# First pair's sums, operand pacing, value stores and late stores moved in a two-layer encoder step

## The chip, the cores and the metric

The kernel runs on one core of a Trainium2 chip. The core has five engines, each with its own in-order queue of instructions: PE (TensorE, matmuls), DVE (VectorE), ACT (ScalarE), POOL (GpSimd) and SP (SyncE, which here only starts transfers). An instruction that has to wait holds back all that stands behind it on its engine. Transfers between the chip's large memory (DRAM below) and the on-chip buffers are started by an engine's queue and run beside the engines. The metric is the device time of one execution in microseconds, the median of three runs.

## The reference

One step of a two-layer streaming encoder on 2048 prompt tokens and 32 sampled tokens, width 1024, in float32. Layer one is a gated delta-rule layer, layer two a banded attention with shared keys and values.

```python
def delta_layer(x, ...):
    proj = x @ w_in                                   # q, k, v, z, a, b
    qkv, new_buf = causal_conv(proj[..., :CONV_DIM], conv_buf, conv_w)
    ...
    o, s_new = gated_delta_rule(q, k, v, g, beta, s0)
    o = o * rsqrt(mean(o * o) + RMS_EPS) * norm_w * silu(z)
    return layer_norm(DN_ALPHA * x + o @ w_out, ln_g, ln_b), new_buf, s_new

def shared_kv(h, w_kv, pos):
    kv = h @ w_kv
    return rope_partial(kv[..., :B_KVW], pos), kv[..., B_KVW:]

def swa_layer(x, k, v, pos, cached, w_in, sinks, w_out, ln_g, ln_b):
    proj = x @ w_in                                   # q and the gate z
    q = rope_partial(proj[..., :B_QW], pos) * (B_HD ** -0.5)
    z = proj[..., B_QW:]
    o = cached_attention(q, k, v, sk) if cached else banded_attention(q, k, v, sk)
    return layer_norm(DN_ALPHA * x + (o * silu(z)) @ w_out, ln_g, ln_b)
```

## The kernel before

Every matrix product in float32 is made of three products of rounded parts: an operand x is split into x_hi (a cast on ACT) and x_lo = x - x_hi (a subtraction on DVE or POOL), and TensorE adds hi·hi, lo·hi and hi·lo. By the trace the stages follow each other: P1 (the first projection with its convolution, to about 690 us), Delta (the delta rule in 17 chunks, to about 1110), O1 (the out-projection with its normalization, to about 1335), P2 (the second projection, q, k, v and gate, about 1310 to 1765) and the attention with its out-projection (to the end).

**O1** takes 17 tiles of 128 tokens (the last has 32). For each, `O1.tiles` fetches the gated output g of the next tile (`g<-s_g`, L1156) and the rows of x (L1161) on SP, splits g (g_hi on ACT, L1168, g_lo on DVE, L1169), multiplies (`po`, L1126 to L1128, two banks), adds the product to the rows (L1134), normalizes, stores h (L1265), turns it on TensorE (L1232) and stores the turned hT (L1236). In this stage PE and DVE run in the order written, and the scheduler orders the others. `more(i)` puts work of P2 between tiles: at tile 8 the split of token block 0, at tile 11 the sums of the first pair.

**P2** multiplies 20 tiles of weights (K: 0 and 1, V: 2 and 3, Q: 4 to 11, Z, the gate: 12 to 19) with five blocks of 416 tokens. Block 0 is multiplied directly ("singles"). Blocks (1, 2) and (3, 4) are two pairs, each multiplied by a scheme of seven products in place of eight (banks X, Z and Y). Its seven operands are b11, b21 and b22, read from hT, and t1 to t4, sums of blocks. Each operand has 4 slices of 128x416. A product is 12 matmuls.

`presum(pair, load, pace)` makes t1 to t4: for each of 4 slices it loads four pieces of hT, makes four subtractions on POOL (L1366) and stores four results (L1370). The first pair's loads are issued by `raw_act` (L1317), the second's by `take_act` (L1352). `operand` casts a slice on ACT (L1400), subtracts on DVE (L1330), and asks for the next slice; 5 slices are held. These steps are chained in `side`: operands of pair 0, sums of pair 1 (with `pace` empty steps before the subtractions), then operands of pair 1, each started as its buffers come free.

`stream` sets the order of P2, where all engines run as written. Before product p it fetches weights 12 products ahead, casts them 3 ahead (w_hi, L1342, ACT) and subtracts 2 ahead (w_lo, L1330, DVE). After the product it takes `STEPS` steps of `side`:

```python
            yield from self.multiply(products[p])
            ...
            for _ in range(self.STEPS):
                next(self.side, None)
            self.settle(self.now)
```

`delay(f, n)` puts f after the product n places on; `settle` calls what is due. K and Q results go through `regroup`: a store to rows (L1671), then copies within DRAM to bq or bk (L1675). V results go through `turn` (L1701): four transpositions into the one bank tp, a copy on ACT into the one buffer v (L1703), and a store to bv (L1704). Gate results go through `finish`: tanh on ACT (L1661), a product on DVE (L1662), a store (L1664).

The last 7 gate tiles of block 0 are multiplied inside the attention, by 14 calls of `gates()`, with a 15th for what is still delayed; `fill(n)` in the attention makes n such calls.

Of the kernel before, what the change touches and what calls it, by code (L numbers as in the profile page):

```python
# [1209 lines left out]
class O1:  # L1210
# [28 lines left out]
    def tiles(self, tiles, ready, more):  # L1239
# [8 lines left out]
        for i, t in enumerate(tiles):  # L1248
            if i == 8:
                yield from more(0)  # L1250
            elif i == 11:
                yield from more(3)
# [21 lines left out]
class P2:  # L1274
# [8 lines left out]
    FETCH, SUM, CAST, SUB, STEPS = 12, 5, 3, 2, 3  # L1283
# [71 lines left out]
    def presum(self, pair, load, pace):  # L1355
# [4 lines left out]
        for k in range(4):  # L1360
            b11, b12, b22, b21 = [load(T["hT"][i, :, b * TB:(b + 1) * TB])
                                  for i, b in ((k, c), (k, d), (4 + k, d), (4 + k, c))]
            for _ in range(pace):
                yield
            for j, (a, b, o) in enumerate(((b12, b11, b11), (b22, b12, b12), (b22, b11, b22), (b21, b22, b21))):
                P.tensor_tensor(out=o[:], in0=a[:], in1=b[:], op=ALU.subtract)  # L1366
                for _ in range(pace // 2):
                    yield
            for n, t in (("t1", b11), ("t3", b12), ("t2", b22), ("t4", b21)):
                self.nc.sync.dma_start(T["sums"][pair, int(n[1]) - 1, k], t[:])  # L1370
                for _ in range(pace // 4):
                    yield
# [151 lines left out]
    def build(self):  # L1524
        self.side = itertools.chain(self.begin(0), *(self.operand(0, n) for n in self.ACTS),
                                    self.presum(1, self.take_act, 12), self.begin(1))
# [45 lines left out]
    def stream(self, products, kept):  # L1572
# [5 lines left out]
        for p in range(-self.FETCH, n):  # L1578
# [11 lines left out]
            if products[p].act:  # L1590
                while products[p].act not in self.have:
                    next(self.side)
# [9 lines left out]

    now, later, side, beside = 0, (), iter(()), iter(())
# [43 lines left out]
    def finish(self, c, i, b):  # L1647
# [11 lines left out]
        else:  # L1659
# [3 lines left out]
                                                              op1=ALU.mult), 2)  # L1663
            self.delay(lambda: nc.sync.dma_start(T["bz"][i - self.Z, :, ts], c[:]), 3)  # L1664

    def regroup(self, c, j, ts, dst, turned):
# [6 lines left out]
        for m, d in enumerate(dst):  # L1673
            src = row[m * n:m * n + n, ts].rearrange("(g r) n -> g r n", r=16)
            self.delay(lambda d=d, src=src: nc.sync.dma_start(d, src), later + 2)  # L1675
# [21 lines left out]
    def turn(self, c, half, b):  # L1697
        nc, w = self.nc, TB // 4
        tp = self.py.tile([128, 4, 128], F32, tag="tp", name="tp")
        for j in range(4):  # L1700
# [3 lines left out]
        self.delay(lambda: nc.sync.dma_start(  # L1704
            self.T["bv"][b * TB:(b + 1) * TB, half * 128:half * 128 + 128].rearrange("(j t) x -> t j x", j=4), v[:w]), 0.5)


class Attention:
# [319 lines left out]
    def run(self, gates, opened):  # L2028
# [77 lines left out]
        for i in range(last):  # L2106
# [7 lines left out]
            elif i % 2 == 0:  # L2114
# [3 lines left out]
                if i + 4 == last:  # L2118
                    self.sampled_keys()
            banks = self.values(order[i], got(i))  # L2120
# [10 lines left out]
            if i < 3:  # L2131
                fill(2)
# [90 lines left out]
def program(tc, I, O, T, G):  # L2223
# [54 lines left out]
    def more(i):  # L2278
        if i == 0:
            p2[0].load0()  # L2280
        elif i == 3:
            drain(p2[0].presum(0, p2[0].raw_act, 0))
# [26 lines left out]
    with tc.manual_schedule(engines={ET.PE, ET.DVE, ET.Activation, ET.Pool, ET.SP}):  # L2309
# [6 lines left out]
        p2.finish_all()  # L2316
    left.close()
# [197 lines left out]
```

## Time and profile before

| | |
|---|---|
| Runs | 2139.36, 2145.09, 2144.28 us; median 2144.28 |
| Profiled execution | 2141.73 us, span 2139.9 us, mean granted TensorE clock 0.986 |
| PE busy | 2052.1 us, 96% of the span |
| DVE, ACT, POOL busy | 68%, 46%, 42% |
| DMA | 360.85 MB, mean 169 GB/s |

The span runs from the first instruction to the last, so 1.8 us of the execution's time lie around it. The busy shares are averages over stages with different limits: what a change in one stage is worth must be read from that stage's windows and waits. A row of waits names an engine and its line, then, after the arrow, what ended its wait.

### The profile page before, as it was taken

To read this page: it belongs to the slowest core of one execution; us is meant where nothing else is said; L and a number is where in the kernel's file an instruction comes from. 1 tells how busy PE (TensorE), PEld (TensorE's weight loads), DVE (VectorE), ACT (ScalarE), POOL (GpSimd) and SP (SyncE) were. 2 spreads that over 40 slices of the span, in tenths; PEclk is the share of its full clock that TensorE was granted. 3 is DMA by queue.
4 is the path that set the end of the run, shared out by engine and by line. 5 is a ranking of instruction groups with operands and counts; after the bars stand their busy time and mean duration, and the time that the engine had idled before them with its cause. 6 is when DMAs were issued, how large, how long until landed. Compare 5 with 4: busy or idle time off the path is not lost.

```text
span 2139.9 us, 37271 instructions
## 1 busy us (share of the span) xinstructions
PE 2052.1 (96%) x13694; PEld 1878.6 (88%) x13694; DVE 1460.8 (68%) x2587; ACT 994.2 (46%) x2466; POOL 894.1 (42%) x1237
## 2 busy tenths in 40 slices
PE   7999999999999999999999989799989998999998
PEld 5999999999999999998987868789979997777775
DVE  4586666666557688888878776668765754566665
ACT  4344444445622376677751201533543446455552
POOL 0132222222132187778722130266445513466666
PEclk9999999999999999999999999999989999999999
DMA  5132333346674545456747684868866658633421
GB/s 203 41 91 77 111 104 99 96 119 208 188 206 152 181 159 176 160 173 224 262 153 254 211 269 127 264 210 264 273 202 199 230 172 275 162 100 99 118 72 65
DMA packets 292633, 360.85 MB, mean 169 GB/s; under 512 B 74130, under 2 KB 217330, under 8 KB 292434
## 3 DMA queue, kind: packets, MB, share of 16 engines
q1 hardware_dynamic: 285394, 341.93, 51.0%
q10 hardware_dynamic: 7056, 16.54, 2.3%
q8 instruction: 108, 1.77, 0.3%
q14 instruction: 75, 0.61, 0.1%
HBM read 235.54 MB, written 134.06 MB: 173 GB/s over the span
## 4 chain that ended last, share of the span: by engine, by line
PE 84%; DMA 9%; DVE 3%; ACT 2%; POOL 1%; issue 1%; SPq 0%; ACTq 0%; DVEq 0%; POOLq 0%
PE ps L79 11%; PE ps L81 11%; PE ps L80 11%; PE ot L1126 3%; PE ot L1127 3%; PE ot L1128 3%; PE X L1638 2%; PE X L1640 2%; PE X L1639 2%; PE S L1978 2%; PE po L1126 2%; PE po L1128 2%; PE po L1127 2%; PE ot L2011 2%; PE tr L1993 2%; PE g L695 1%
## 5 line engine op out<-in xcount | busy, mean ns | idle before, releaser
L79 PE MATMUL ps<-act_hi,w_hi 128*128 128x416 f32 x1280 | 455.0, 355 | 0.8 <-ACT w_hi L55 0.8
L81 PE MATMUL ps<-act_hi,w_lo 128*128 128x416 f32 x1280 | 450.1, 352 | 0.0
L80 PE MATMUL ps<-act_lo,w_hi 128*128 128x416 f32 x1280 | 447.9, 350 | 0.0
L79 PEld LDWEIGHTS ps<-act_hi,w_hi 128*128 128x128 f32 x1280 | 240.3, 188 | 5.0 <-ACT w_hi L55 1.2
L80 PEld LDWEIGHTS ps<-act_lo,w_hi 128*128 128x128 f32 x1280 | 240.6, 188 | 3.0
L81 PEld LDWEIGHTS ps<-act_hi,w_lo 128*128 128x128 f32 x1280 | 240.1, 188 | 3.3
L209 DVE SCALAR_TENSOR_TENSOR y<-R,convw,y 128x2083 f32<-128x2083 f32 x72 | 184.8, 2568 | 62.3 <-ACT y L206 46.3
L56 POOL TENSOR_TENSOR w_lo<-w_raw,w_hi 128x1024 fp32r<-128x1024 f32 x25 | 61.7, 2469 | 330.0 <-ACT w_hi L55 304.7
L1812 POOL TENSOR_TENSOR P<-e,sm 128x384 f32<-128x384 f32 (+2 forms) x128 | 102.0, 818 | 170.0 <-DVE sm L1802 119.4
L729 POOL TENSOR_TENSOR tm<-L,Tt 128x60 f32<-128x60 f32 (+19 forms) x365 | 130.7, 358 | 82.1 <-issue 39.8
L1330 DVE TENSOR_TENSOR w_lo<-w_raw,w_hi 128x512 fp32r<-128x512 f32 x132 | 133.0, 1026 | 35.8 <-ACT w_hi L1342 35.8
L731 POOL TENSOR_TENSOR Tt<-Tt,tm 128x60 f32<-128x60 f32 (+19 forms) x365 | 142.6, 391 | 28.6
L1798 ACT ACTIVATE e<-S,nm 128x193 f32<-128x193 f32 (+2 forms) x260 | 104.8, 416 | 90.4 <-DVE nm L1793 53.3
L1126 PE MATMUL po<-wo_hi,g_hi 128*128 128x512 f32 x256 | 104.2, 407 | 12.6 <-DVE r L1134 12.4
L305 ACT COPY R<-ps 128x416 f32<-128x416 f32 (+1 forms) x144 | 60.3, 442 | 107.9 <-PE ps L81 92.8
L1470 ACT ACTIVATE o<-X 128x416 f32<-128x416 f32 x80 | 41.5, 519 | 137.9 <-PE X L1640 137.9
L1126 PE MATMUL ot<-wo,g_hi 128*128 128x512 f32 x256 | 103.8, 405 | 1.5 <-DMA wo<-s_wob 1.5
L1128 PE MATMUL po<-wo_hi,g_lo 128*128 128x512 f32 x256 | 100.7, 393 | 0.5 <-DVE g_lo L1169 0.5
L1127 PE MATMUL ot<-wo,g_hi 128*128 128x512 f32 x256 | 100.8, 394 | 0.0
L1128 PE MATMUL ot<-wo,g_lo 128*128 128x512 f32 x256 | 100.8, 394 | 0.0
L1127 PE MATMUL po<-wo_lo,g_hi 128*128 128x512 f32 x256 | 100.2, 391 | 0.0
L1342 ACT CAST w_hi<-w_raw 128x512 fp32r<-128x512 f32 x140 | 83.5, 616 | 27.3 <-DMA w_raw<-in_b_w 10.8
(361 smaller groups left out, 5113.6 us busy)
## 6 DMA issues: line engine op xcount, KB each, us to landing
w_raw<-in_b_w SPq DMA_DIRECT2D x60, 512.0 KB
w_raw<-in_w_in SPq DMA_DIRECT2D x40, 512.0 KB
act_raw<-s_hT SPq DMA_DIRECT2D x64, 208.0 KB
s_rows<-o SPq DMA_DIRECT2D x50, 208.0 KB
k<-s_k SPq DMA_DIRECT2D x17, 512.0 KB
E<-s_E SPq DMA_DIRECT2D x17, 512.0 KB
s_bq<-s_rows SPq DMA_DIRECT2D x40, 208.0 KB
s_bz<-o SPq DMA_DIRECT2D x40, 208.0 KB
```

What stands on the lines that cost most here:

```text
L79: nc.tensor.matmul(ps, hi[:, k, :], xh[:, k, :], start=(k == 0), stop=False)
L80: nc.tensor.matmul(ps, hi[:, k, :], xl[:, k, :], start=False, stop=False)
L81: nc.tensor.matmul(ps, lo[:, k, :], xh[:, k, :], start=False, stop=(k == KC - 1))
L209: nc.vector.scalar_tensor_tensor(out=y[:], in0=R[:, j:j + W], scalar=self.convw[:, i, j:j + 1], in1=y[:], op0=ALU.mult, op1=ALU.add)
L729: P.tensor_tensor(out=tm[:n, i0 - k:, :w], in0=L[:n, i0:, j:j + 1].to_broadcast(sh), in1=Tt[:n, j:j + 1, :w].to_broadcast(sh), op=ALU.mult)
L731: P.tensor_tensor(out=Tt[:n, i0:, :w], in0=Tt[:n, i0:, :w], in1=tm[:n, i0 - k:, :w], op=ALU.subtract)
L1126: nc.tensor.matmul(ps[:n], ghi[:, k, :n], hi, start=a, stop=False)
L1127: nc.tensor.matmul(ps[:n], ghi[:, k, :n], lo, start=False, stop=False)
L1128: nc.tensor.matmul(ps[:n], glo[:, k, :n], hi, start=False, stop=z)
L1330: P.tensor_tensor(out=lo, in0=raw, in1=hi, op=ALU.subtract)
L1798: self.nc.scalar.activation(x.e[:, h, u, :x.n], x.S[:, h, u, :], AF.Exp, bias=x.nm[:, h, u:u + 1], scale=1.0, accum_out=x.sm[:, h, u:u + 1])
L1812: self.nc.gpsimd.tensor_tensor(out=x.P[:, u, :nj * 128].rearrange("r (j h k) -> r j h k", h=2, k=64), in0=x.e[:, :, u, :n].rearrange("r h ...
```

## The change

Five places are edited. `more(3)` at tile 11 becomes four calls at tiles 11 to 14, each of one slice of the first pair's sums. `STEPS` goes from 3 to 2, and the empty steps in the second pair's sums from 12 to 6. The copies in `regroup` come three products later. The store of v is issued by ACT right behind its copy, where SP issued it half a step later. The late gates' product and store come one step later each, and the closing call of `fill` moves ahead of `values` at the third attention tile.

```diff
@@ -1248,8 +1248,8 @@
         for i, t in enumerate(tiles):
             if i == 8:
                 yield from more(0)
-            elif i == 11:
-                yield from more(3)
+            elif 11 <= i < 15:
+                yield from more(i - 8)
             while not all(ready(u) for u in tiles[i + 1:i + 2]):
                 yield 1.0
             ahead = self.fetch(*tiles[i + 1]) if i + 1 < len(tiles) else None
@@ -1280,7 +1280,7 @@
 
 
     K, V, Q, Z = 0, 2, 4, 12
-    FETCH, SUM, CAST, SUB, STEPS = 12, 5, 3, 2, 3
+    FETCH, SUM, CAST, SUB, STEPS = 12, 5, 3, 2, 2
     EARLY, LATE = 4, 2
     HELD = 5
     PAIRS = (1, 2), (3, 4)
@@ -1352,12 +1352,12 @@
         self.nc.sync.dma_start(t[:], src)
         return t
 
-    def presum(self, pair, load, pace):
+    def presum(self, pair, load, pace, slices=range(4)):
 
 
         c, d = self.PAIRS[pair]
         P, T = self.nc.gpsimd, self.T
-        for k in range(4):
+        for k in slices:
             b11, b12, b22, b21 = [load(T["hT"][i, :, b * TB:(b + 1) * TB])
                                   for i, b in ((k, c), (k, d), (4 + k, d), (4 + k, c))]
             for _ in range(pace):
@@ -1523,7 +1523,7 @@
 
     def build(self):
         self.side = itertools.chain(self.begin(0), *(self.operand(0, n) for n in self.ACTS),
-                                    self.presum(1, self.take_act, 12), self.begin(1))
+                                    self.presum(1, self.take_act, 6), self.begin(1))
 
     def then(self, p, gen):
 
@@ -1589,7 +1589,7 @@
                 continue
             if products[p].act:
                 while products[p].act not in self.have:
-                    next(self.side)
+                    next(self.side, None)
                 next(self.beside, None)
             yield from self.multiply(products[p])
             if products[p].after:
@@ -1600,6 +1600,7 @@
             self.now += 1
             yield 1.13
 
+    late = False
     now, later, side, beside = 0, (), iter(()), iter(())
 
     def settle(self, until):
@@ -1660,8 +1661,8 @@
             t = self.out()
             self.delay(lambda: nc.scalar.activation(t[:], c[:], AF.Tanh), 1)
             self.delay(lambda: nc.vector.scalar_tensor_tensor(out=c[:], in0=t[:], scalar=1.0, in1=c[:], op0=ALU.add,
-                                                              op1=ALU.mult), 2)
-            self.delay(lambda: nc.sync.dma_start(T["bz"][i - self.Z, :, ts], c[:]), 3)
+                                                              op1=ALU.mult), 3 if self.late else 2)
+            self.delay(lambda: nc.sync.dma_start(T["bz"][i - self.Z, :, ts], c[:]), 4 if self.late else 3)
 
     def regroup(self, c, j, ts, dst, turned):
 
@@ -1672,7 +1673,7 @@
         n = 128 // len(dst)
         for m, d in enumerate(dst):
             src = row[m * n:m * n + n, ts].rearrange("(g r) n -> g r n", r=16)
-            self.delay(lambda d=d, src=src: nc.sync.dma_start(d, src), later + 2)
+            self.delay(lambda d=d, src=src: nc.sync.dma_start(d, src), later + 5)
 
     def load_tables(self):
         if self.turned:
@@ -1701,8 +1702,8 @@
             nc.tensor.transpose(tp[:w, j, :], c[:, j * w:j * w + w], self.ident[:, :])
         v = self.tab.tile([128, 4, 128], F32, tag="v", name="v")
         nc.scalar.copy(v[:w], tp[:w])
-        self.delay(lambda: nc.sync.dma_start(
-            self.T["bv"][b * TB:(b + 1) * TB, half * 128:half * 128 + 128].rearrange("(j t) x -> t j x", j=4), v[:w]), 0.5)
+        nc.scalar.dma_start(
+            self.T["bv"][b * TB:(b + 1) * TB, half * 128:half * 128 + 128].rearrange("(j t) x -> t j x", j=4), v[:w])
 
 
 class Attention:
@@ -2117,6 +2118,8 @@
                     self.gate(order[i + 4])
                 if i + 4 == last:
                     self.sampled_keys()
+            if i == 2:
+                fill(1)
             banks = self.values(order[i], got(i))
             gated = self.gated(order[i], banks, c)
             largest(i + 1, 1)
@@ -2128,7 +2131,7 @@
             largest(i + 2, 0)
             exps(i + 2, 0)
             shares(i + 1, 1)
-            if i < 3:
+            if i < 2:
                 fill(2)
             if po:
                 self.product(po, c, 0)
@@ -2278,8 +2281,8 @@
     def more(i):
         if i == 0:
             p2[0].load0()
-        elif i == 3:
-            drain(p2[0].presum(0, p2[0].raw_act, 0))
+        elif i >= 3:
+            drain(p2[0].presum(0, p2[0].raw_act, 0, (i - 3,)))
         else:
             yield from p2[0].go(4 * i)
 
@@ -2314,6 +2317,7 @@
         p2.beside = p2.out_weights()
         drain(p2.go(p2.left))
         p2.finish_all()
+        p2.late = True
     left.close()
     spare.close()
     att = Attention(tc, left, I, O, T, G)
```

Three places in the order of the engines follow. Names are outputs, then inputs; x2 means two in a row.

SP in the out-projection, at the sums of the first pair (L1317 loads, L1370 stores of sums; L1156 the next tile's g, L1161 its x, L1265 and L1236 the stores of h and hT). The end of the block before:

```order
L1317 DMA act_raw<-s_hT 128x416
L1236 DMA s_hT<-hT 128x8x128
L1370 DMA s_sums<-act_raw 128x416
L1317 DMA act_raw<-s_hT 128x416
L1370 DMA s_sums<-act_raw 128x416
L1156 DMA g<-s_g 128x1024
L1370 DMA s_sums<-act_raw 128x416 x2
L1265 DMA s_h<-r 128x1024
L1370 DMA s_sums<-act_raw 128x416 x4
```

and the beginning of the same block now:

```order
L1317 DMA act_raw<-s_hT 128x416 x6
L1370 DMA s_sums<-act_raw 128x416
L1317 DMA act_raw<-s_hT 128x416 x2
L1265 DMA s_h<-r 128x1024
L1370 DMA s_sums<-act_raw 128x416 x2
L1156 DMA g<-s_g 128x1024
L1370 DMA s_sums<-act_raw 128x416
L1317 DMA act_raw<-s_hT 128x416 x2
L1370 DMA s_sums<-act_raw 128x416
```

The fetch of g stood behind 26 of the block's 32 transfers; it now stands behind 11, and a second one behind 15 more. The block still ends within two more stores of hT.

ACT at the beginning of P2 (L1342 casts of weights, L1400 casts of operand slices, L1427 evictions of singles). Before:

```order
L1400 CAST b11h<-act_raw 128x416 x2
L1400 CAST b21h<-act_raw 128x416
L1342 CAST w_hi<-w_raw 128x512
L1400 CAST b21h<-act_raw 128x416 x3
L1342 CAST w_hi<-w_raw 128x512
L1427 ACTIVATE o<-ps 128x416
L1400 CAST t2h<-act_raw 128x416 x3
L1342 CAST w_hi<-w_raw 128x512
```

Now:

```order
L1400 CAST b11h<-act_raw 128x416
L1400 CAST b21h<-act_raw 128x416
L1342 CAST w_hi<-w_raw 128x512
L1427 ACTIVATE o<-ps 128x416
L1400 CAST b21h<-act_raw 128x416 x2
L1342 CAST w_hi<-w_raw 128x512
L1400 CAST b21h<-act_raw 128x416
L1400 CAST t2h<-act_raw 128x416
```

Between two casts of weights stand two operand slices instead of three, so the 28 slices of a pair reach over 14 products instead of about 9.

ACT at the values of the first pair (in the changed file the lines of `turn` are one higher, and L1470 is an eviction of X). Before:

```order
L1703 COPY v<-tp 104x512
L1342 CAST w_hi<-w_raw 128x512
L1703 COPY v<-tp 104x512
L1342 CAST w_hi<-w_raw 128x512
L1470 ACTIVATE o<-X 128x416
L1703 COPY v<-tp 104x512
```

Now:

```order
L1704 COPY v<-tp 104x512
L1705 DMA s_bv<-v 104x4x128
L1342 CAST w_hi<-w_raw 128x512
L1704 COPY v<-tp 104x512
L1705 DMA s_bv<-v 104x4x128
L1342 CAST w_hi<-w_raw 128x512
L1470 ACTIVATE o<-X 128x416
L1704 COPY v<-tp 104x512
L1705 DMA s_bv<-v 104x4x128
```

Each copy is followed by its store on the same queue, ahead of the next cast of weights. The order of PE's instructions is the same in both kernels.

## The prediction

> **What bounds the kernel now.** I read the first and fourth parts of the page first, to see which engine sets the end, then busy times by window over the whole span, then the waits of TensorE, and then what its releasers themselves waited for.
>
> ```profile
> PE 2052.1 (96%) x13694; PEld 1878.6 (88%) x13694; DVE 1460.8 (68%) x2587; ACT 994.2 (46%) x2466; POOL 894.1 (42%) x1237
> PE 84%; DMA 9%; DVE 3%; ACT 2%; POOL 1%; issue 1%; SPq 0%; ACTq 0%; DVEq 0%; POOLq 0%
> ```
>
> TensorE is busy 96% of the span and holds 84% of the chain. The edit removes no matmul, so it can pay only where TensorE stands still. The 9% of DMA in the chain is the place to look. By windows the holes are few (columns: sum of the window, PE busy with its count of matmuls, PEld, DVE, ACT, POOL, granted clock, DMA share, GB/s):
>
> ```profile
> 1260.00:1280.00 20.00, 10.20 (x43) 8.16 (x43) 9.56 (x21) 2.68 (x3) 7.90 (x7) 0.74 0.95 338
> 1280.00:1290.00 10.00, 10.00 (x50) 8.27 (x49) 6.67 (x14) 1.64 (x2) 0.00 (x0) 1.00 0.49 147
> 1340.00:1380.00 40.00, 28.15 (x123) 24.82 (x122) 24.46 (x44) 22.52 (x46) 4.29 (x3) 0.90 0.82 268
> 1410.00:1420.00 10.00, 5.08 (x17) 4.75 (x17) 2.07 (x4) 3.15 (x6) 3.24 (x3) 0.66 0.76 249
> 1530.00:1570.00 40.00, 31.13 (x152) 28.83 (x151) 30.84 (x52) 24.62 (x52) 6.73 (x4) 0.91 0.78 249
> 1570.00:1580.00 10.00, 10.00 (x55) 9.90 (x53) 3.35 (x7) 4.00 (x8) 2.69 (x2) 1.00 0.59 178
> 1580.00:1590.00 10.00, 6.66 (x23) 6.05 (x22) 6.40 (x10) 1.64 (x3) 5.69 (x4) 0.69 0.63 210
> 1620.00:1630.00 10.00, 6.07 (x26) 5.57 (x25) 2.49 (x4) 3.15 (x6) 4.62 (x4) 0.83 0.67 190
> ```
>
> The undisturbed rows give the pace: 50 matmuls in 10 us in the out-projection (0.20 us each, row 1280) and 55 in the second projection (0.182 us each, row 1570; a product of 12 is 2.18 us). Matmuls missing against that pace, times the pace, are the time lost, and this counts the slow clock after a hole too, which idle time alone leaves out. 1260:1280 misses 57, 11.4 us. 1340:1380 misses 97 of 220, 17.6 us. 1410:1420 misses 38, 6.9. 1530:1570 misses 68, 12.4. 1580:1590 misses 32, 5.8. 1620:1630 misses 29, 5.3. That is 59.4 us in six places. The waits of TensorE between 1230 and 1700 name who ends each (us in total, times, longest):
>
> ```profile
> PE po L1126 <- DVE r L1134: 9.8, 1, 9.8
> PE ps L1640 <- DVE w_lo L1330: 5.2, 3, 3.3
> PE X L1638 <- ACT o L1470: 4.7, 2, 4.2
> ...
> PE tp L1701 <- ACT v L1703: 8.8, 2, 4.9
> PE ps L1640 <- DVE w_lo L1330: 8.0, 3, 5.2
> PE Z L1640 <- DVE w_lo L1330: 3.3, 1, 3.3
> ```
>
> None of these releasers is slow itself; each stands on its own in-order queue behind something that waits for a transfer. The steps below follow each back to that transfer.
>
> **A, first pair's sums over four tiles of the out-projection.** The 9.8 us hole, traced upstream, by timeline:
>
> ```profile
> 1236.99 0.32 SPq L1156 DMA_DIRECT2D g<-s_g  x1
> ...
> 1264.63 0.48 SPq L1156 DMA_DIRECT2D g<-s_g  x1
> ...
> 1270.58 1.04 ACT L1168 CAST g_hi<-g 128x1024 fp32r<-128x1024 f32 x1 [2.23 <-DMA g<-s_g]
> ...
> 1271.66 1.23 DVE L1169 TENSOR_TENSOR g_lo<-g,g_hi 128x1024 fp32r<-128x1024 f32 x1 [9.95 <-ACT g_hi L1168]
> ```
>
> Two fetches of g stand 27.6 us apart: on SP 26 of the 32 sum transfers (16 loads, 16 stores) and 5 others were issued between them, 0.89 us each. The fetch landed 5.95 us after issue, DVE stood 9.95 us at that g_lo, and the addition that frees TensorE's bank stands behind it. A tile takes about 10.5 us (48 matmuls at 0.20 and the transpositions), so the fetch was 17.1 us late against that rhythm and TensorE 9.8: 7.3 us is the slack. After, by the order, the 32 transfers still stand in nearly one block, but the fetch of g stands behind 11 of them, with 3 others (12.5 us, 2 over), and the next one behind 15 more, with 3 others (16.0 us, 5.5 over): 7.5 us late together, against a slack of 7.3. Against a clean result stands the transfers' own limit: 6.8 MB (32 of 208 KB) must go through within some two tiles, and 338 GB/s at a DMA share of 0.95 is what they reached. I take 2.4 us as left, gain 9 (bounds 0, if the second g is as late as the first was, and 11.4).
>
> **B and D, operands at two slices a product.** 28 slices of a pair pass through a load, a cast on ACT (L1400) and a subtraction on DVE (L1330), all in the same queues as the weights' casts:
>
> ```profile
> L1400 ACT CAST b11h<-act_raw x8: 527/540/542, 1338.9 to 1534.1; 128x416 fp32r<-128x416 f32 x8
> L1400 ACT CAST b22h<-act_raw x8: 528/538/542, 1368.2 to 1566.9; 128x416 fp32r<-128x416 f32 x8
> ...
>   DMA act_raw<-s_hT: 19.0, 9
>   DMA act_raw<-s_sums: 16.6, 8
> ...
> 1374.79 0.54 ACT L1400 CAST b22h<-act_raw 128x416 fp32r<-128x416 f32 x1 [3.74 <-DMA act_raw<-s_hT]
> ```
>
> A cast takes 0.54 us, and yet the casts of pair 0 run from 1338.9 to 1374.8: 27 steps in 35.9 us, 1.33 each, and those of pair 1 come at 24 steps in 32.8 us (1534.1, the fourth of b11h, to 1566.9), 1.37. ACT waited 35.6 us at them for loads, both pairs together. So a pair needs some 37 us, whatever the program asks. At three steps a product it asks for them in 28/3 = 9.3 products, 20.3 us: 16.7 too few, and the weights behind them come late (17.6 lost in B, 12.4 in D). At two it asks in 14 products, 30.5 us: 6.5 too few. B then keeps 6.5 of its 17.6, gain 11 (bounds 0 and 17.6). For D the weights are cast three products ahead, two of which (4.4 us) can be eaten: 16.7 - 4.4 = 12.3, just the 12.4 found, so after it keeps 6.5 - 4.4 = 2.1, gain 10.2 (bounds 0 and 12.4). What is late next is the load itself: the DMA share is 0.82 and 0.78 there while TensorE runs at 56% and 69% of its pace, so at full pace the transfers come near their limit. DVE (30.84 of 40 us in D) is the other near limit. Spread wider, b22 and t4 are made while the group's first products run; each still stands ahead of its product, and a missing one is drawn forward by the loop in the stream.
>
> The pair-1 sums wait 6 instead of 12 steps between load and subtraction and, at two steps a product, run over fewer products. That puts more POOL work beside DVE's:
>
> ```profile
> 1385.00:1530.00 145.00, 140.08 (x737) 138.10 (x736) 107.91 (x119) 60.70 (x119) 94.25 (x62) 0.98 0.76 244
> SPq L1675 <- DMA s_rows<-o: 80.7, 37, 5.3
> L1675 SPq DMA_DIRECT2D s_bq<-s_rows x40: 613/630/753, 1318.1 to 1694.5; - x40
> PE ot L1126 <- DMA wo<-s_wob: 1.5, 1, 1.5
> ```
>
> I cost it at nothing: DVE has 37 us free of those 145 and POOL 51. If that cover goes, w_lo comes late as it does in D.
>
> Regrouping three products later (6.5 us) takes SP's 80.7 us of waits for its own stores away, the longest 5.3, so 6.5 covers them. SP is in front of every load, but its wait shows in no PE row except through B and D: nothing of its own. Its last one moves from 1694.5 to 1701, and attention begins after 1760.
>
> **C, values stored from ACT's queue.** There is one buffer for v and one bank for tp, so a transposition waits for the copy before, and that for the store before it:
>
> ```profile
> 1406.90 7.42 DMA s_bv<-v
> ...
> ACT v L1703 <- DMA s_bv<-v: 24.0, 5, 8.1
> ...
> 1405.23 0.59 ACT L1703 COPY v<-tp 104x512 f32<-104x512 f32 x1 [1.72 <-issue]
> ...
> 1414.42 0.59 ACT L1703 COPY v<-tp 104x512 f32<-104x512 f32 x1 [8.09 <-DMA s_bv<-v]
> ...
> 1417.99 0.59 ACT L1703 COPY v<-tp 104x512 f32<-104x512 f32 x1 [2.05 <-DMA s_bv<-v]
> ...
> 1415.06 1.09 PE L1701 MATMUL tp<-ident,o 128*104 128x128 f32 x4 [4.92 <-ACT v L1703]
> 1624.24 0.69 PE L1701 MATMUL tp<-ident,o 128*104 128x128 f32 x4 [3.93 <-ACT v L1703]
> ...
> 1567.93 6.44 DMA s_bv<-v
> ...
> 1575.55 6.88 DMA cs<-in_cs
> ```
>
> The stores took 7.42 and 6.44 us behind other transfers of SP's, while the one after the copy of 1414.42 was done by 1417.99, 3 us after that copy's end. A store on ACT's queue stands right behind its copy and not behind loads and sums. The new wait: its issue can be held by an earlier transfer's completion, and then the casts of w_hi behind it stand too. I take 4 us a store instead of 7.4, the end nearest to the 3 us row, as the queue behind which it then stands is nearly empty. The hole of 4.92 shrinks to about 1.5, short enough for the clock (below), and the 3.93 one to 0.5; gains 5.4 of 6.9 and 4.8 of 5.3, less 1.8 for held issues: 8.4 (bounds 0 and 12.2; a loss is rival 4).
>
> The chain through 1584 hangs on the same store: SP stood at a store of v whose copy waited for the store of 1567.93, and the table load behind it (1575.55) ended in the w_lo of that hole. Without the store on SP it can start some 5 us sooner: 4.5 of 5.8 (bounds 0 and 5.8).
>
> The Trainium skill, page "DMA: Bandwidth & Descriptors", section "Issuing engines are not separate DMA queues", says that transfers started by different engines run on the same 16 engines and interleave, and that another issuer saves only issue time; by it C and the table would give about 1.1 us (the store's 1406.90 less the end of its copy, 1405.82) and not 12.9, and the sum would be 12 us smaller. The same page, section "Queues, rings and completion order", says that each of the 16 takes packets from its rings in turn, which would let a lone store pass a backlog; no run here yet shows which decides.
>
> Clock:
>
> ```profile
> 1555.08 0.71 PE L1640 MATMUL ps<-act_hi,w_lo 128*128 128x416 f32 x1 [5.22 <-DVE w_lo L1330]
> 1564.69 0.46 PE L1640 MATMUL ps<-act_hi,w_lo 128*128 128x416 f32 x1 [2.22 <-DVE w_lo L1330]
> ```
>
> After the hole of 5.22 the matmul took 0.71 us, after 2.22 us 0.46: holes cut below some 2 us cost their own length only, so what stays is priced without a slow clock.
>
> **E, late gates.** Of the last gate tiles the product and the store come one step later, and the closing step is drawn ahead of the values of the third attention tile. PE's order is unchanged; the only hole near is the 1.5 us for wo, which is loaded behind these stores. 0.5 (bounds -2, if DVE's softmax work stands behind the product, and 1.5).
>
> **The sum.** 9 + 11 + 10.2 + 8.4 + 4.5 + 0.5 = 43.6. The profiled execution took 2141.73 us (span 2139.9, 1.8 around it): 2098.1. It lies 2.55 below the median of the three runs, 2144.28; on that scale 2100.7, 2101.
>
> **Rivals.** (1) Transfers or DVE limit the operands whatever their spacing, and B and D give half: 10.6 less, 2111. For it speaks the DMA share of 0.82 at a halting TensorE; against it, the lag that two steps leave is 6.5 and not 16.7. With nothing from them, 2122. (2) The sums are spread in name only: the 32 transfers still stand in one block of SP, and the second fetch of g is late: 9 less, 2110; 15 transfers ahead of the second fetch speak for it. (3) The stores land no sooner: C and the table give 1.1, 11.8 less, 2113. (4) Slower: ACT blocks. Ten stores each hold ACT's queue, with the weights' casts behind it, until another transfer is done; at the longest transfer seen, 7.42, all on the path, that costs 74 us, against 30.7 from A, B, D and E: 2144.28 + 74.2 - 30.7 = 2188. It decides from 3.1 us a store on. Against it: only what passes the 4.4 us cover of early casts reaches TensorE, 3.0 of 7.4 us.
>
> **How the numbers follow.** Forecast 0.50, rival 1 0.18, rival 2 0.09, rival 3 0.12, rival 4 0.06, and 0.05 that gains and new waits cancel. About 0.3%, 6.4 us, is what a measurement here tells from no change. Faster 0.88 (the forecast and rivals 1 to 3, less 0.01), same 0.06, slower 0.06. The low end is all 59.4 and 0.5 gone, 2084; the high end takes rivals 1 and 2 or 1 and 3 together (2120, 2123) and some of C's held issues: 2128.
>
> **What would show it.** Right: no wait of po for r near 1265; 1340:1380 with about 185 matmuls and the 28 casts of L1400 wider apart on ACT; no PE wait at tp above 2 us; SP's wait at the regrouping nearly gone; PE's busy share of the span up to 97 or 98%. Wrong if the hole comes back one tile later, if w_lo waits stay at 5 us and more while the DMA share goes to 0.95 (rival 1), if s_bv still takes 6 us (rival 3), or if ACT's queue shows long waits at the store of v with w_hi late behind it (rival 4).

## The result, and the profile after

The changed kernel took 2122.51 us (median of 4 runs, 2119.34 to 2124.99) against 2144.69 for the kernel before: 22.2 us, a ratio of 0.9898 with a 95% interval of 0.9872 to 0.9924. The forecast was 2101, a gain of 43.6, with a range of 2084 to 2128. The direction was right and half of the gain came.

The profiled execution is the slowest of the four (2124.99), so against the profiled execution before (2141.73) only 16.7 us can be looked for in the two traces. First the page's busy line, then the windows at the six places of the prediction, in the columns shown there:

```profile
PE 2050.3 (97%) x13694; PEld 1876.3 (88%) x13694; DVE 1461.3 (69%) x2587; ACT 995.1 (47%) x2466; POOL 905.0 (43%) x1237
```

```profile
1260.00:1290.00 30.00, 25.14 (x111) 20.31 (x110) 22.55 (x44) 3.27 (x4) 9.48 (x8) 0.94 0.85 291
1340.00:1380.00 40.00, 31.23 (x130) 27.96 (x129) 26.66 (x39) 21.21 (x42) 10.21 (x6) 0.83 0.77 245
1400.00:1420.00 20.00, 13.89 (x69) 13.32 (x68) 7.92 (x12) 6.56 (x13) 7.65 (x7) 0.83 0.68 213
1470.00:1500.00 30.00, 28.88 (x149) 27.31 (x149) 25.06 (x24) 13.61 (x27) 22.00 (x15) 1.00 0.84 284
1530.00:1560.00 30.00, 25.81 (x128) 23.79 (x127) 24.17 (x41) 18.64 (x39) 5.79 (x5) 0.94 0.83 265
1580.00:1590.00 10.00, 10.00 (x56) 9.86 (x55) 7.41 (x9) 3.44 (x7) 7.10 (x5) 1.00 0.79 260
1600.00:1620.00 20.00, 16.12 (x75) 15.39 (x74) 6.71 (x12) 6.10 (x12) 5.18 (x4) 0.83 0.52 158
```

At the same pace (0.20 us a matmul in the first row, 0.182 in the others) the time still lost is 7.8 us at the sums (11.4 before), 16.4 at the first pair's operands (17.6), 7.5 and 6.4 at the two transpositions (6.9 and 5.3), 6.7 at the second pair's operands with 2.9 more at 1470:1500 (12.4 in all before), and nothing at 1580 (5.8). That gives 3.6 + 1.2 - 0.6 - 1.1 + 2.8 + 5.8 = 11.7. The wait for wo of 1.5 us near 1800 is gone too. Of the other 3.5 us, 2.4 are no part of the change: at 1230, before the first edited place has run, the changed kernel's trace is already 12 matmuls ahead (8670 against 8658, at 0.20 us each). The waits of TensorE (1230 to 1400, then 1400 to 1700):

```profile
PE po L1126 <- DVE r L1134: 4.9, 2, 4.4
PE ps L1641 <- DVE w_lo L1330: 3.2, 1, 3.2
PE X L1641 <- DVE w_lo L1330: 2.7, 2, 2.2
PE X L1639 <- ACT t3h L1400: 1.8, 1, 1.8
...
PE tp L1702 <- ACT v L1704: 10.0, 2, 6.1
PE ps L1641 <- DVE w_lo L1330: 3.8, 2, 2.8
```

The holes of w_lo are shorter, the one at po is halved, and the waits at tp, which the store on ACT was to close, have grown from 8.8 to 10.0 us. By these windows alone the spacing of the operands seems worth some 4 us (1.2 at the first pair and 2.8 at the second). The experiments show that this reading is wrong: parts of the change depend on each other.

### The profile page after: what moved, and what is told of

It is laid out like the page before. It is cut to its first block, busy times and chain, and to the rows that moved or that the text cites. A ratio compares the mean times of both kernels' runs of the same rounds, so it can differ in the third digit from the quotient of the medians.

```text
span 2123.0 us, 37258 instructions
## 1 busy us (share of the span) xinstructions
PE 2050.3 (97%) x13694; PEld 1876.3 (88%) x13694; DVE 1461.3 (69%) x2587; ACT 995.1 (47%) x2466; POOL 905.0 (43%) x1237
## 5 line engine op out<-in xcount | busy, mean ns | idle before, releaser
L56 POOL TENSOR_TENSOR w_lo<-w_raw,w_hi 128x1024 fp32r<-128x1024 f32 x25 | 71.5, 2861 | 329.1 <-ACT w_hi L55 285.4
L1470 ACT ACTIVATE o<-X 128x416 f32<-128x416 f32 x80 | 41.5, 519 | 130.1 <-PE X L1641 127.7
L1342 ACT CAST w_hi<-w_raw 128x512 fp32r<-128x512 f32 x140 | 83.5, 616 | 34.0 <-DMA w_raw<-in_b_w 16.1
```

## The experiments

Each is the changed kernel with the edit shown, unless it says that it starts from the kernel before. All were run against the kernel before, in three sets (1 to 4, 5 to 8, 9 to 12), each on one chip.

| Kernel | Median us | Ratio to before, 95% interval |
|---|---|---|
| changed | 2122.51 | 0.9898, 0.9872 to 0.9924 |
| 1, three operand steps | 2140.19 | 0.9990, 0.9973 to 1.0006 |
| 2, three steps for the first pair | 2129.84 | 0.9945, 0.9928 to 0.9962 |
| 3, store of v on SP | 2116.22 | 0.9881, 0.9861 to 0.9901 |
| 4, turns apart | 2110.84 | 0.9858, 0.9839 to 0.9877 |
| 5, sums at tile 11 | 2127.75 | 0.9929, 0.9906 to 0.9953 |
| 6, regrouping at 2 | 2135.63 | 0.9967, 0.9952 to 0.9983 |
| 7, turns apart, store on SP | 2111.47 | 0.9857, 0.9832 to 0.9883 |
| 8, turns apart, early loads | 2106.38 | 0.9837, 0.9812 to 0.9862 |
| 9, before with two steps | 2156.33 | 1.0057, 1.0036 to 1.0078 |
| 10, before with regrouping at 5 | 2135.60 | 0.9956, 0.9937 to 0.9976 |
| 11, pace 12 and gates as before | 2145.52 | 1.0012, 0.9995 to 1.0029 |
| 12, as 8, sums' loads on ACT | 2113.02 | 0.9856, 0.9823 to 0.9888 |

Every kernel here lies within 2% of the kernel before. The microseconds given below between two rows of the table are differences of medians. The kernel before had medians of 2144.69 beside the changed kernel and 2142.99, 2141.07 and 2143.84 in the three sets, so a difference between sets is uncertain by some 2 to 4 us. Where the intervals of two ratios overlap, the difference is not told from noise: this holds for 3 and 5 against the changed kernel, and for 7, 8 and 12 against 4 or 8. Those of 4 and the changed kernel just touch (0.9877 and 0.9872), while their runs lie apart: the slowest of 4 is 2113.10, the fastest of the changed kernel 2119.34.

**1. Three operand steps again.**

```diff
-    FETCH, SUM, CAST, SUB, STEPS = 12, 5, 3, 2, 2
+    FETCH, SUM, CAST, SUB, STEPS = 12, 5, 3, 2, 3
```

> The changed kernel with three operand steps a product again (everything else as changed). By the windows after the change, two steps gave about 2 us at the first pair (1340:1380 lost 17.6 us before, 15.8 after) and about 4 at the second: 2122.5 + 6 = 2128 to 2130. By the prediction's own terms (11 and 10.2) it would be 2143. If the spacing has no effect at all because transfers alone set the rate: 2120 to 2125.

It lost 17.7 us, nearly all of the gain: more than four times the 4 us of the windows, three times the 6 us of the expectation, and nearer to the 21.2 us of the prediction's own terms. One part of it is not at the operands at all: the hole of the transpositions, 6.1 us in the changed kernel, is 10.8 here.

```profile
1420.15 1.09 PE L1702 MATMUL tp<-ident,o 128*104 128x128 f32 x4 [10.80 <-ACT v L1704]
```

**2. Three steps for the first pair alone.**

```diff
-            for _ in range(self.STEPS):
+            for _ in range(3 if self.now < 40 else 2):
```

> Three steps a product up to product 40 and two behind it, so that only the first pair's operands are made as before. Theory that the first pair is limited by its loads: 2122 to 2125, with 1340:1380 still near 130 matmuls. Theory of the prediction (spacing, 11 us): 2133. The second pair keeps its gain in both.

7.3 us slower than the changed kernel: between the two expectations. The windows 1330:1385, this kernel first and the changed one second:

```profile
1330.00:1385.00 55.00, 40.88 (x190) 37.31 (x189) 34.53 (x52) 27.06 (x55) 14.80 (x10) 0.94 0.80 254
...
1330.00:1385.00 55.00, 46.23 (x209) 42.83 (x208) 35.40 (x55) 28.43 (x57) 12.18 (x7) 0.88 0.81 257
```

19 matmuls at 0.182 make 3.5 us at the operands themselves. The hole at tp is 10.8 us here too, 4.7 more. So the spacing of the first pair is worth some 3.5 us at its own place, and the rest shows at the store of v behind it. The difference to experiment 1, 10.3 us, is the second pair with its sums.

**3. The store of v on SP again.**

```diff
-        nc.scalar.dma_start(
-            self.T["bv"][...], v[:w])
+        self.delay(lambda: nc.sync.dma_start(
+            self.T["bv"][...], v[:w]), 0.5)
```

> The store of v from SP again, half a product late (everything else as changed). If the store is slow on either queue, the wait of the transpositions for the copy of v stays near 9 to 10 us and only the table load behind the store on SP comes late again: 2126 to 2129, with a hole of 3 us at the w_lo behind the table. If the store on ACT did bring 8.4 us beside that, as predicted: 2135. If holding ACT cost more than it saved: 2115 to 2120.

6.3 us faster by the medians, in the third range of the expectation; the intervals overlap, so that this part of the change costs time is likely and not shown. That it gains 8.4 us, as forecast, is ruled out: the ratio would then be about 0.994, outside the interval. The waits at tp fall from 10.0 to 4.3 us with the store on SP:

```profile
PE tp L1702 <- ACT v L1704: 4.3, 2, 3.8
```

The two traces show how. On ACT (the changed kernel), copies, stores and the transposition that waited:

```profile
1398.75 0.59 ACT L1704 COPY v<-tp 104x512 f32<-104x512 f32 x1 [2.79 <-DMA s_bv<-v]
1401.53 0.35 ACTq L1705 DMA_DIRECT2D s_bv<-v  x1
...
1408.07 0.59 ACT L1704 COPY v<-tp 104x512 f32<-104x512 f32 x1 [5.48 <-DMA s_bv<-v]
...
1408.71 1.09 PE L1702 MATMUL tp<-ident,o 128*104 128x128 f32 x4 [6.11 <-ACT v L1704]
```

and the chain in the changed kernel at the second such hole, then the chain with the store on SP at the first:

```profile
1593.16 6.95 DMA s_bk<-s_rows
...
1600.13 0.02 ACTq L1705
...
1600.19 6.56 DMA s_bv<-v
...
1398.05 7.33 DMA s_bv<-v
```

On ACT the copy of 1398.75 ended at 1399.34, and its store was issued 2.2 us later, at 1401.53; the row does not say what it waited for. At 1600, where the issue came 1.0 us after its copy, the chain says it: a regrouping copy of 6.95 us, issued by SP, had to finish first. Then the two stores took 6.2 and 6.6 us. On SP it was issued within 0.05 us of its copy's end and took 7.33. So the transfer is slow on either queue, and ACT adds a wait for a transfer that has nothing to do with the store. The Trainium skill, page "DMA: Bandwidth & Descriptors", section "Issuing engines are not separate DMA queues", states that another issuing engine saves issue time only, since all transfers run on the same 16 engines; the trace agrees that the transfer is no faster (6.2 and 6.6 us against 7.33), and here the issue even came later.

**4. Turns at least four products apart.**

```diff
-            self.delay(lambda: self.turn(c, i - self.V, b), 2)
+            at = max(self.now + 2, self.next_turn)
+            self.next_turn = at + 4
+            self.delay(lambda: self.turn(c, i - self.V, b), at - self.now)
```

> The changed kernel with two turns of values at least four products (8.7 us) apart, where they came as close as one product. If the two holes at tp (6.1 and 3.9 us idle, some 13 us with the slow clock behind them) come from a store of 6 us out of the one buffer of v, they go and nothing takes their place: 2110 to 2113. If the held ACT queue is the cause (the weights' casts behind a store that waits for another transfer), the tp waits go but waits for w_lo or X appear: 2117 to 2122. If the results, held longer in their buffers, stop the evictions: 2122 or more.

11.7 us faster, with no wait at tp left, as the first expectation had it. The longest waits of TensorE between 1400 and 1700 are then:

```profile
PE ps L1641 <- DVE w_lo L1330: 4.3, 2, 3.6
PE X L1641 <- DVE w_lo L1330: 1.2, 2, 0.6
```

The cause of both holes is that values are turned as close as one product (2.2 us) apart while their one buffer needs 6 to 7 us to be stored. A second buffer should do the same; no run here has one.

**5. The first pair's sums in one call at tile 11.**

```diff
-            elif 11 <= i < 15:
-                yield from more(i - 8)
+            elif i == 11:
+                yield from more(3)
...
-            drain(p2[0].presum(0, p2[0].raw_act, 0, (i - 3,)))
+            drain(p2[0].presum(0, p2[0].raw_act, 0))
```

> The changed kernel with the first pair's sums called in one go at tile 11 again. By the windows (1260:1290 lost 11.4 us before, 7.0 to 7.8 after) the call by slices is worth some 4 us: 2126, with the single hole of 9 to 10 us back. By the prediction's term 9: 2131. If the order around the sums does not matter, since the transfers are the limit: 2122.

5.2 us slower by the medians, though the intervals overlap: nearer to the first expectation (4) than to the prediction's 9. The single hole is back:

```profile
1268.72 0.76 PE L1126 MATMUL po<-wo_hi,g_hi 128*128 128x512 f32 x1 [9.82 <-DVE r L1134]
```

**6. The regrouping copies at 2 again.**

```diff
-            self.delay(lambda d=d, src=src: nc.sync.dma_start(d, src), later + 5)
+            self.delay(lambda d=d, src=src: nc.sync.dma_start(d, src), later + 2)
```

> The changed kernel with the regrouping copies two products behind their store again, not five. If SP's waits there were covered (the prediction, nothing of its own): 2122 to 2124. If they delay operand loads and stores, they return to SP (80 us in all, up to 5.3 each) and w_lo and the table come late again: 2128 to 2134, with the hole near 1584 back. If a later copy has a price of its own (more transfers at the bad moment): below 2120.

13.1 us slower. SP's waits are back, and TensorE has 37 matmuls (6.7 us) fewer in 1385:1530, with waits of 4.4 us at X for an eviction (o, L1470) between 1400 and 1700 against 0.5 in the changed kernel (this kernel first, the changed one second):

```profile
SPq L1676 <- DMA s_rows<-o: 77.2, 34, 6.0
...
1385.00:1530.00 145.00, 132.12 (x678) 128.56 (x677) 94.44 (x109) 58.74 (x114) 90.38 (x61) 0.95 0.73 237
...
1385.00:1530.00 145.00, 136.71 (x715) 133.02 (x715) 108.58 (x122) 63.45 (x126) 90.85 (x62) 0.98 0.76 254
```

The hole of 1584 did not come back here, so that part of the expectation failed.

**7. Turns apart, store on SP** (3 and 4 together).

> Turns at least four products apart and the store of v on SP. With the turns apart the store is off the path on either queue; what is left of ACT's queue is the time that its casts stand behind a store held by another transfer. If that is hidden by the early casts: 2109 to 2112, as with the store on ACT (2110.8). If it reaches TensorE: 2104 to 2107. If SP is the worse place once the copies no longer wait: 2113 or more.

2111.47, as with the store on ACT (2110.84): once no copy waits for a store, no difference between the two queues can be told.

**8. Turns apart, and five early loads** (4, and the first operand loads of the first pair issued ahead of the last stores of the out-projection).

```diff
+            if i == 2:
+                p2[0].first_loads()
...
+    def first_loads(self):
+        parts = [(0, name, k) for name in self.ACTS for k in range(4)]
+        self.coming = [self.raw_act(self.source(*x)) for x in parts[:self.HELD]]
+        self.first = parts[self.HELD:]
```

> Turns four products apart, and the first five operand loads of the first pair issued at the end of the out-projection (into the buffers of the results) instead of behind its last stores. Between 1290 and 1330 the DMA share is 0.24 to 0.36, behind it 0.83 to 0.94. If the first pair waits for its transfers (the 5 loads that come early are 6.5 us of it), 1340:1380 gains 5 to 7: 2104 to 2106. If it waits for something else (DVE beside POOL, the sums' loads): 2109 to 2112. If the results lack the five buffers: 2113 or more.

4.5 us faster than 4 by the medians, though the intervals overlap, and the lowest median of all: 2106.38. Against the changed kernel the intervals stand apart. In 1330:1385 it has 234 matmuls against 217 in experiment 4 and 209 in the changed kernel, and the hole at ps (2.2 and 3.2 us there) is gone:

```profile
1330.00:1385.00 55.00, 47.95 (x234) 44.91 (x233) 37.64 (x60) 28.95 (x58) 12.60 (x8) 0.94 0.78 244
```

What stays there is a wait of 2.4 us for t3 and 2.2 us for w_lo, much as in the changed kernel (1.8 and 2.2).

**9. The kernel before with two operand steps alone.**

```diff
-    FETCH, SUM, CAST, SUB, STEPS = 12, 5, 3, 2, 3
+    FETCH, SUM, CAST, SUB, STEPS = 12, 5, 3, 2, 2
```

> The kernel before with two operand steps a product alone (no other part of the change). If the spacing carries its gain by itself: some 14 to 18 us faster, 2126 to 2130 (putting it back in the changed kernel cost 17.7). If it needs the later regrouping and the shorter steps of the second pair's sums, because at two steps the second pair's sums and operands end too late: 2135 to 2143 or slower, with holes at X or Z between 1530 and 1600 where an operand is drawn forward.

12.5 us slower than the kernel before. The spacing does not carry a gain by itself. At the first pair it does gain, 215 matmuls in 1330:1385 against 197 in the kernel before (3.3 us), near the 3.5 us of experiment 2:

```profile
1330.00:1385.00 55.00, 45.28 (x215) 40.10 (x213) 35.45 (x61) 27.25 (x56) 10.21 (x6) 0.94 0.72 226
```

The loss lies at the second pair, where TensorE stands for 10.6 us before its first product; experiment 11 shows why.

**10. The kernel before with the regrouping at 5 alone.**

```diff
-            self.delay(lambda d=d, src=src: nc.sync.dma_start(d, src), later + 2)
+            self.delay(lambda d=d, src=src: nc.sync.dma_start(d, src), later + 5)
```

> The kernel before with the regrouping copies three products later alone. Going back cost 13 us in the changed kernel. If that is a gain of its own (SP no longer stands behind its own stores): 2129 to 2133, with the hole of 1584 gone. If the later copies only help where the store of v stands on ACT, whose issue waits for an earlier copy: 2140 to 2144.

8.2 us faster, between the two expectations. A one-line move that was costed at nothing is worth more than a third of the whole gain. All of it lies in 1575:1700, where it has 45 matmuls (8.2 us) more (this kernel first, the kernel before second):

```profile
1575.00:1700.00 125.00, 122.53 (x651) 119.95 (x650) 91.69 (x108) 50.95 (x98) 75.05 (x46) 1.00 0.69 227
...
1575.00:1700.00 125.00, 117.73 (x606) 115.42 (x605) 80.99 (x101) 48.58 (x95) 66.76 (x41) 0.96 0.66 213
...
1584.16 0.46 PE L1640 MATMUL X<-b11h,w_lo 128*128 128x416 f32 x1 [1.08 <-DVE w_lo L1330]
```

Near 1584, where TensorE stood for 3.34 us, it now stands for 1.08, and the second hole at tp, 3.93 us before, is 0.61. These are two of the holes that the prediction gave to the store on ACT; here they close with the store still on SP.

**11. The two parts costed at next to nothing, put back.**

```diff
-    self.presum(1, self.take_act, 6)
+    self.presum(1, self.take_act, 12)
...
-        p2.late = True
...
-            if i == 2:
-                fill(1)
...
-            if i < 2:
+            if i < 3:
                 fill(2)
```

> The changed kernel with the two parts costed at nothing and at 0.5 us put back: 12 empty steps in the second pair's sums, and the late gates and the closing call as before. If the prediction is right on both: 2121 to 2125, with the wait for wo of 1.5 us back near 1800. If the sums end too late for the second pair at two steps a product: 2130 or more, with operands waiting for the sums' transfers at 1530 to 1600. If less POOL work beside DVE gains something: below 2119.

23 us slower, and no faster than the kernel before (the interval reaches from 0.9995 to 1.0029). TensorE in this kernel, then the POOL subtractions of the sums (first and last start) in the changed kernel, in this one, and in experiment 9:

```profile
1558.28 0.71 PE L1639 MATMUL X<-b11h,w_hi 128*128 128x416 f32 x1 [11.20 <-ACT b11h L1400]
```

```profile
L1366 POOL TENSOR_TENSOR act_raw<-act_raw x32: 1065/1206/2637, 1246.8 to 1484.9; 128x416 f32<-128x416 f32 x32
...
L1366 POOL TENSOR_TENSOR act_raw<-act_raw x32: 1058/1089/2110, 1243.3 to 1550.5; 128x416 f32<-128x416 f32 x32
...
L1366 POOL TENSOR_TENSOR act_raw<-act_raw x32: 1058/1084/1537, 1250.4 to 1567.9; 128x416 f32<-128x416 f32 x32
```

The sums of the second pair stand ahead of its operands in the same chain of steps. At two steps a product and 12 empty steps they end at 1550 instead of 1485, the operands begin behind them, and TensorE stands 11.2 us before the second pair's first product. The late gates were put back in the same kernel and were not measured apart; in the trace no hole of theirs beyond the 0.9 us wait for wo is seen. The shorter pace has a price too: in 1385:1530 this kernel has 737 matmuls against 715 in the changed kernel, 4.0 us by these two traces.

**12. As 8, with the loads of the first pair's sums on ACT's queue.**

```diff
-            drain(p2[0].presum(0, p2[0].raw_act, 0, (i - 3,)))
+            drain(p2[0].presum(0, p2[0].act_load, 0, (i - 3,)))
...
+    def act_load(self, src):
+        t = self.wk.tile([128, TB], F32, tag="o", name="act_raw")
+        self.nc.scalar.dma_start(t[:], src)
+        return t
```

> The version with turns four products apart and five early loads (2106.4), and the loads of the first pair's sums issued on ACT's queue, so that SP's fetch of g stands behind their stores alone. If the hole of 4 us at 1278 comes from the place of the fetch on SP: it goes, 2100 to 2103. If the transfers' own limit (share 1.0 there) makes it: it stays or moves, 2105 to 2108. If ACT's queue is held by the loads and the casts of g_hi come late: 2109 or more.

2113.02, no gain over 8: 6.6 us slower by the medians, with overlapping intervals. That is in the third range of the expectation, yet the cast of g_hi waited for g here and not for ACT's queue. The hole stays, one tile earlier and longer. SP, ACT and TensorE in this kernel, and the window (DMA share 1.05):

```profile
1260.40 0.60 SPq L1156 DMA_DIRECT2D g<-s_g  x1
...
1267.78 1.04 ACT L1168 CAST g_hi<-g 128x1024 fp32r<-128x1024 f32 x1 [1.16 <-DMA g<-s_g]
...
1270.98 0.77 PE L1126 MATMUL po<-wo_hi,g_hi 128*128 128x512 f32 x1 [4.89 <-DVE r L1134]
...
1260.00:1270.00 10.00, 6.09 (x31) 4.83 (x30) 5.74 (x5) 1.63 (x2) 7.29 (x6) 0.93 1.05 366
```

g took 7.4 us from issue to its cast. That fits the transfers' own limit. But SP's stores of sums still stand ahead of the fetch, so the two causes are not separated and stay open.

## Why the prediction was half right

The time lies inside the range, but in part by luck: the regrouping, priced at nothing, brought what C failed to bring. It also meets the 2122 of rival 1 with nothing from B and D, and that is chance: experiment 1 shows that the spacing matters (17.7 us), though it gains only together with the shorter sums. Of its signs of being right, the single wait at 1265 went, and so did SP's waits at the regrouping; but 130 matmuls stand in 1340:1380 where it named 185, and TensorE waits up to 6.1 us at tp where it named 2.

**A, the sums (forecast 9, measured 5.2 by undoing it, 3.6 by the windows).** The fetch of g did come early, as worked out: a hole of 0.5 us at the first tile. One tile later a hole came back, the prediction's own sign of being wrong and in part its rival 2. The step that failed is the slack of 7.3 us for the second: it followed g alone, and the rows of x had moved too. The changed kernel on ACT, SP and DVE:

```profile
1272.01 1.05 ACT L1168 CAST g_hi<-g 128x1024 fp32r<-128x1024 f32 x1 [8.72 <-DMA g<-s_g]
...
1271.16 0.52 SPq L1161 DMA_DIRECT2D r<-in_x  x1
...
1277.39 0.69 DVE L1134 SCALAR_TENSOR_TENSOR r<-r,po 128x512 f32<-128x512 f32 x1 [3.08 <-DMA r<-in_x]
```

g was split by 1274.3. The fetch of x left SP only at 1271.16, behind the sums, and the addition that frees the bank waited 3.08 us more for it: the hole of 4.36 at 1278. Every tile needs two transfers, and the estimate had priced one.

**B, the first pair (forecast 11, measured 7.3, of which 3.5 at its own place).** The term that was mis-sized is what remains, 6.5 us by the forecast; 16.4 us remain. It took the time that a pair's slices need as fixed, and that time grew. (At two steps a product the program itself asks for the slices later, so the spacing is part of the growth.) The casts in the changed kernel:

```profile
L1400 ACT CAST b11h<-act_raw x8: 532/540/545, 1332.6 to 1518.1; 128x416 fp32r<-128x416 f32 x8
...
L1400 ACT CAST b22h<-act_raw x8: 536/538/543, 1366.7 to 1555.6; 128x416 fp32r<-128x416 f32 x8
```

From the first of b11h to the first of b22h they take 34.1 us for 24 steps, 1.42 each, where the same two rows before give 29.3 us and 1.22. One load kept ACT waiting for 5.7 us (b21, to 1344.97) behind two weight transfers that SP issued at 1336.46, and experiment 8 got that back. Of the rest, a collision can be seen that the prediction had only at pair 1's sums. DVE and POOL in the changed kernel:

```profile
1365.31 5.52 DVE L1330 TENSOR_TENSOR t4l<-act_raw,t4h 128x416 fp32r<-128x416 f32 x2
...
1364.30 2.03 POOL L1690 TENSOR_TENSOR o<-o,cs 64x416 f32<-64x416 f32 x1 [12.14 <-DMA s_bq<-s_rows]
...
1370.35 2.73 POOL L1454 TENSOR_TENSOR w_raw<-w_raw 128x512 f32<-128x512 f32 x1
```

Two subtractions took 5.52 us where each takes 0.58 alone, while POOL worked without a break from 1364.3 to 1373.1. Before, this run of POOL began at 1377, when the last operand had been made; at two steps a product the operands reach into it. In all ten kernels that make the first pair at two steps, one of the t4 subtractions takes 3.9 us; in the four at three steps (before, 1, 2 and 10), where POOL's run begins after them, none takes over 1.5 us. The Trainium skill, page "SBUF — State Buffer", section "Who interferes with whom", states that a VectorE instruction with two inputs in SBUF, the on-chip memory, contends with a GpSimd instruction that reads SBUF, over a port pair that acts as an exclusive lock; these rows agree, and no run here took POOL's work away to prove it or to price it.

The prediction also priced what stays without a slow clock, since holes below 2 us had cost none. That step failed. TensorE in the changed kernel:

```profile
1365.44 0.71 PE L1641 MATMUL X<-b11h,w_lo 128*128 128x416 f32 x1 [0.47 <-DVE w_lo L1330]
...
1371.99 0.71 PE L1641 MATMUL X<-t4h,w_lo 128*128 128x416 f32 x1 [2.22 <-DVE w_lo L1330]
1376.27 0.69 PE L1639 MATMUL Z<-b22h,w_hi 128*128 128x416 f32 x1 [0.45 <-DVE o L1475]
...
1370.00:1380.00 10.00, 7.57 (x26) 6.79 (x27) 8.86 (x14) 4.22 (x8) 3.07 (x2) 0.66 0.67 182
```

The matmuls take 0.71 us after holes of 0.47 and 2.22, and the granted clock is 0.66, with no hole above 2.3 us within 15 us. In this trace several small holes close together went with as slow a clock as one large one had. In experiment 9 it was 0.83 from 1370 to 1390, again with no hole above 2.22 us.

**C and the table (forecast 8.4 and 4.5).** C failed: by the medians the store on ACT costs 6.3 us (experiment 3). The step that failed is the 4 us a store, taken because the queue would be nearly empty: 6.2 and 6.6 was measured at the two holes. Held issues, priced at 1.8 for all, were 2.2 at a single store. Rival 3 held for the duration, and rival 4's mechanism held at a small size. The table's hole did go, and not through ACT's queue alone: with the store back on SP (3) no hole above 1 us is there either, and the regrouping alone (10) cuts it from 3.34 to 1.08 us.

**D, the second pair (forecast 10.2, measured 10.3 as the difference of experiments 1 and 2).** The size agrees, in part by luck: 9.6 us are still lost there where 2.1 were to remain, and of the 10.3 us only 27 matmuls (4.9 us) lie in 1530:1590, where experiment 1 has 257 and experiment 2 has 284. The account of what it needs was wrong. The shorter pace of the sums was costed at nothing, with only its load on POOL in view. Without it the spacing alone turns into a loss (9), and the gain of the whole change is gone (11). What was to be priced is when the sums end, since the operands stand behind them in the same chain.

**Regrouping (forecast nothing of its own).** It is worth 8.2 us alone and 13.1 in the changed kernel. The step that failed is that SP's 80.7 us of waits reach TensorE through B and D only: alone (10) they showed at the table's w_lo and at tp, and in the changed kernel (6) at X. That SP issued what stands behind its waits late is the likely way; it was not followed instruction by instruction.

**E, the late gates (forecast 0.5).** The wait for wo of 1.5 us is gone, and 0.9 of it is back in experiment 11; the part was not measured apart.

**The sum.** The terms add up only if each can be had alone. Undone one by one, spacing, pace with the late gates, regrouping and sums cost 17.7, 23, 13.1 and 5.2 us, and the store returns 6.3; that is far more than the 22.2 they gave together, since without one the others give less.

## What to carry to other kernels

When work is made at fewer steps a product, price the whole chain that shares these steps, from the first item to the deadline of the last: here two steps alone lost 12.5 us and two steps with a shorter chain gained. A single buffer that is stored over 6 to 7 us sets a least distance between its uses, and moving the uses apart gained 11.7 us where moving the store to another queue gained nothing. A queue's waits that name no one on the bounding engine need not be free (8.2 us here): look who stands behind the waiting instruction.

## What the runs showed of the hardware

A store of v (208 KB) took 6.2 to 7.4 us where a copy was held up by it, from either queue, and some 3 us elsewhere; ACT issued one 2.2 us after its copy, and in a second place an issue on ACT waited for a transfer that SP had started. Holes of 0.5 to 2.2 us close together went with a granted clock of 0.66, as a single hole of 4.9 us had before. Two subtractions of 0.58 us on DVE took 5.52 us beside a steady run of POOL.
